# The output projection of a hybrid backbone layer, its operands split into float16 halves with power-of-two scales

## The chip, the core and the metric

The kernel runs on one core of one Trainium2 chip. The metric is device time in microseconds of one execution; a time is the median over the runs made. The engines are named as in the profile: PE multiplies matrices (PEld is its weight load, which runs beside it), DVE is the vector engine, ACT the scalar engine, POOL the GpSimd engine, SP the engine that issues most DMAs. Each engine takes its own instructions in the order in which they were written for it.

## What is computed

One layer over 4096 latent tokens of width 1024, with 256 context tokens ahead of them. An input projection gives eight groups of 512 columns: query q, two forget gates, value v, the gate g_a, the convolution's u and its gate, and the gate g_b. Two branches follow, and one output projection joins them:

```python
a_lat = rmsnorm(h_lat, norm_g[l]) * (1.0 + sc_l) + sh_l
q_l, zf_l, zb_l, v_l, ga_l, u_l, ug_l, gb_l = jnp.split(a_lat @ w_in[l], SPLITS, axis=-1)
...
branch_a = head_rmsnorm(o_hgrn, hgrn_norm_g_l) * jax.nn.silu(g_a)
branch_b = conv_y * jax.nn.silu(g_b)      # conv_y = silu(layernorm(depthwise conv of width 31))
out_lat = jnp.concatenate([branch_a, branch_b], axis=-1) @ w_out_l
...
h_lat = h_lat + gt_l * out_lat
return rmsnorm(h_lat, final_norm_g)
```

o_hgrn is a gated linear recurrence run forward and backward over the tokens; gt_l is a row of 1024 gates that depends on c alone. Everything is float32 in the reference.

## The kernel before

**Two stages.** Stage 1 walks forward over 16 blocks of 256 tokens. In a block, `hgrn` (the forward scan and the within-chunk scores), `row_conv` and the projections of the next block are interleaved by `merge`, which takes the next step of whichever generator is least far along; a scheduler then lists the instructions of each engine in the order in which they come ready in its own simulation, so that a DMA or a small step can move ahead of its place in the code. Results that stage 2 needs go to DRAM (`opd`, `qbd`, `ubd`, `yrd`, `gud`, `aTd`). Stage 2 walks backward over 32 groups of 128 tokens: `group_in` finishes the backward scan of a group (`pi`, `ps_c`, `ps_d`, `ps_o` are its PE steps), applies the norms and gates, and makes the operand of the output projection; `group_out` does the output projection of the group before it (`py`), the residual and the final norm; `gates` and `col_conv` of a later block run beside them.

**Splits.** Most matrix products run on two halves, high and low, in three passes (high by high, high by low, low by high; `PASSES`). For the input projection the halves are float16, with a power-of-two scale from the sum of squares (`exponent`, `split_chunk`). For the output projection (`split_wo` at line 896, the end of `group_in`, `group_out`) the halves are float32r: `yh = round(y)`, `yl = y - yh`, 4 bytes each. A group has 2 halves of 512 output columns x 3 passes x 8 chunks = 48 matmuls of 128x128 by 128x512.

**Side work.** A dictionary `side` (line 916) hangs preparation on blocks of stage 1: block 1 computes the gate row (`gate_rows`), block 2 measures the two gate weights (`scale_w2`: 8 loads of 512 KB, 8 squares on ACT, two small reductions through PE), blocks 3 to 6 split them (`split_w2`), blocks 7 to 10 fold gate and norm gain into w_out and split it (`split_wo`, two rows k per block, two halves each: two loads, a multiply on DVE, a copy on ACT, a subtract on DVE, two stores). Blocks 11 to 13 have no side work. The side tiles share the one buffer with tag "A" with the preparation of x two blocks ahead (`prep_rows`).

**Weights of stage 2.** `load_w2` loads the high halves of w_out (2 MB, into the place of weights no longer used) in block 15; the low halves, 4 MB in four DMAs from POOL's queue, are loaded at line 1175 into tiles of stage 2's own pool `m2`, which lies over the tiles of stage 1's pool `m1`.

`rsqrt` is one instruction on DVE and then 12 (for 4 columns) or 7 (for one column) small ones on POOL, in a chain.

## Time and profile before

| | |
|---|---|
| median of 3 runs | 2219.68 us (2218.23 to 2222.2) |
| the profiled execution's own time | 2215.77 us |
| its span, first to last instruction | 2214.0 us |
| PE / PEld busy in the span | 2083.6 us (94%) / 1642.5 us (74%) |
| DVE / ACT / POOL busy | 1749.6 (79%) / 996.3 (45%) / 458.5 us (21%) |
| mean granted PE clock | 0.978 of full speed |
| HBM read / written | 137.99 MB / 76.55 MB |

The profiled execution is a single one; 1.77 us of its time lie outside the span. Start times in the rows are microseconds from the span's start. Stage 1 ends near 1433, stage 2 runs from there to 2214. "idle before <- X" is time in which an engine stood still until X came.

### The profile page before, as it was taken

Reading aid. Unit: us, or ns where it says so; the run is one execution under the profiler, and the core shown is the slowest. Engines: PE = TensorE matmul, PEld = TensorE weight load, DVE = VectorE, ACT = ScalarE, POOL = GpSimd, SP = SyncE. Lnnn points to the kernel's source line nnn. Section 1 sums busy time; section 2 is a strip of 40 time slices with the busy share of each in tenths; the row PEclk is TensorE's granted clock in tenths of the full one; section 3 lists DMA queues with packets and bytes.
Section 4 is the critical chain, followed back from the end, with each engine's and each line's share of the span. In section 5 each row is a group of like instructions: output and inputs, shape, how many; then the busy total and the mean of one; then the engine's idle time right before and its main releaser. Section 6 shows DMA issues by size and latency. Waiting matters only on the chain. (4 is left out here: it accounts for less than half of the span.)

```text
span 2214.0 us, 54678 instructions
## 1 busy us (share of the span) xinstructions
PE 2083.6 (94%) x22334; PEld 1642.5 (74%) x22334; DVE 1749.6 (79%) x4270; ACT 996.3 (45%) x2310; POOL 458.5 (21%) x1146
## 2 busy tenths in 40 slices
PE   6999999999998999999999999978999999999997
PEld 3777778778777778778788876766677766667776
DVE  5988887897797887887898778888787887777754
ACT  4944545545535445445544543433333333333343
POOL 1110101110110110101110100044433344433332
PEclk8999999999999999999999999989999999999999
DMA  9436165324325335343322317332323322332322
GB/s 363 133 84 163 55 169 149 104 79 134 102 68 177 109 99 172 98 115 97 85 61 68 64 59 234 107 130 94 110 91 108 102 96 91 100 98 99 114 96 72
DMA packets 221476, 251.65 MB, mean 114 GB/s; under 512 B 143812, under 2 KB 147736, under 8 KB 216744
## 3 DMA queue, kind: packets, MB, share of 16 engines
q1 hardware_dynamic: 220104, 239.67, 36.4%
q0 software_dynamic: 1120, 8.49, 1.0%
q8 instruction: 175, 2.87, 0.5%
q14 instruction: 77, 0.63, 0.1%
HBM read 137.99 MB, written 76.55 MB: 97 GB/s over the span
## 5 line engine op out<-in xcount | busy, mean ns | idle before, releaser
L284 PEld LDWEIGHTS <-w 128*128 128x128 f16 x4704 | 455.8, 98 | 60.5 <-issue 2.6
L706 DVE SCALAR_TENSOR_TENSOR yr<-gu,convw,yr 128x224 f32<-128x224 f32 (+2 forms) x900 | 356.6, 444 | 0.0
L1048 DVE SCALAR_TENSOR_TENSOR ycs<-gu_all,convw,ycs 128x256 f32<-128x256 f32 (+2 forms) x828 | 343.9, 469 | 0.0
L284 PEld LDWEIGHTS <-pair 128*128 128x128 f16 x3168 | 308.5, 99 | 39.4 <-issue 0.6
L1146 PE MATMUL py<-wo,yh 128*128 128x512 f32 x1024 | 282.1, 413 | 3.8 <-ACT yh L1130 3.8
L81 POOL TENSOR_SCALAR xqh<-xssq 128x1 f32<-128x1 f32 x30 | 12.5, 418 | 1017.7 <-DVE xssq L257 1017.7
L1146 PEld LDWEIGHTS py<-wo,yh 128*128 128x128 f32 x1024 | 189.0, 192 | 43.8 <-ACT yh L1130 4.4
L284 PE MATMUL ps_z<-aT,pair 128*128 128x256 f16 x1632 | 191.1, 277 | 0.0
L1015 PE MATMUL ps_gb<-aT,w 128*128 128x256 f16 x1536 | 190.1, 273 | 0.0
L284 PE MATMUL ps_z<-aT,w 128*128 128x256 f16 x1632 | 188.3, 274 | 1.9 <-DVE aT L242 1.4
L295 PE MATMUL pv<-w,aT 128*128 128x512 f16 x816 | 184.4, 379 | 1.4 <-DVE gu L670 1.4
L751 ACT COPY km<-X 128x512 f32<-128x512 f32 x160 | 107.9, 675 | 168.2 <-DVE X L759 167.9
L284 PE MATMUL ps_u<-aT,w 128*128 128x256 f16 x1536 | 180.6, 274 | 0.0
L1003 PE MATMUL ps_ga<-w,aT 128*128 128x512 f16 x768 | 178.6, 385 | 0.0
L284 PE MATMUL ps_g<-aT,w 128*128 128x256 f16 x1536 | 178.3, 273 | 0.0
L284 PE MATMUL ps_q<-aT,pair 128*128 128x256 f16 x1536 | 172.9, 273 | 0.0
L1015 PEld LDWEIGHTS <-w 128*128 128x128 f16 x1536 | 145.5, 98 | 31.5 <-issue 15.8
L295 PEld LDWEIGHTS <-aT 128*128 128x128 f16 x816 | 77.4, 98 | 88.3 <-issue 1.6
L1146 PE MATMUL py<-wo,yl 128*128 128x512 f32 x512 | 139.6, 402 | 0.0
L1003 PEld LDWEIGHTS <-aT 128*128 128x128 f16 x768 | 72.8, 99 | 88.1 <-issue 10.4
L314 ACT ACTIVATE f<-f,lbv,oml 128x128 f32<-128x128 f32 x272 | 113.0, 485 | 0.1
L1146 PEld LDWEIGHTS py<-wo,yl 128*128 128x128 f32 x512 | 95.0, 192 | 19.1
(268 smaller groups left out, 3360.7 us busy)
## 6 DMA issues: line engine op xcount, KB each, us to landing
xt<-in_x_dram SPq DMA_DIRECT2D x64, 512.0 KB, 3.5
out_dram<-xt SPq DMA_DIRECT2D x31, 512.0 KB, 2.7
aTd<-aT SPq DMA_DIRECT2D x14, 1024.0 KB, 4.7
aT<-aTd SPq DMA_DIRECT2D x14, 1024.0 KB, 5.8
wst<-in_w_in_dram SPq DMA_DIRECT2D x16, 512.0 KB, 4.5
wod<-hl SPq DMA_DIRECT2D x32, 256.0 KB, 3.0
qbd<-X SPq DMA_DIRECT2D x31, 256.0 KB, 2.1
ubd<-ub SPq DMA_DIRECT2D x31, 256.0 KB, 2.0
```

What stands on the lines that cost most here:

```text
L81: eng.tensor_scalar(h, v, -0.5, 0.0, ALU.mult, ALU.add)
L284: nc.tensor.matmul(ps[:, j, :], w[:, wi, k, (ct + j) * P : (ct + j + 1) * P], aT[:, ai, k, :], start=n == 0, stop=n == 23)
L295: nc.tensor.matmul(pv, aT[:, ai, k, i * P : (i + 1) * P], W[G_V][:, wi, k, :], start=n == 0, stop=n == 23)
L314: nc.scalar.activation(fa, fa, AF.Identity, scale=oml[:, d, ct + j : ct + j + 1], bias=lbv[:, d, ct + j : ct + j + 1])
L706: nc.vector.scalar_tensor_tensor(ar[i][:, :, lo:hi], gr[i][:, :, lo + dl : hi + dl], convw[:, i, j : j + 1], ar[i][:, :, lo:hi], ALU.mult, ...
L751: nc.scalar.copy(fap(km, 0, kd), fap(Xs[gi], 0, ks))
L1003: nc.tensor.matmul(ps, aT[:, ai, k, i * P : (i + 1) * P], Wa[:, wi, k, :], start=n == 0, stop=n == 23)
L1015: nc.tensor.matmul(ps[:, j, :], Wb[:, wi, k, (ct + j) * P : (ct + j + 1) * P], aT[:, ai, k, :], start=n == 0, stop=n == 23)
L1048: nc.vector.scalar_tensor_tensor(ya, gu_all[:, i, (lo + dl) * GW : (hi + dl) * GW], convw[:, 2 + i, j : j + 1], ya, ALU.mult, ALU.add)
L1146: nc.tensor.matmul(py, y[:, k // 4, k % 4, :], W2[wi, nh][:, k, :], start=n == 0, stop=n == 23)
```

## The change

The halves of both operands of the output projection become float16. For that they need scales that keep them in float16's range: `wo_scales`, a new piece of side work in block 7, loads w_out once more, sums its squares, and works out from bounds (largest norm gains, gate weights' sums of squares, the shift and scale of the modulation, the largest gate) two power-of-two scales for y (`ky`), two for w_out (`kw`, `khg`), and one factor that undoes them (`kinv`). `gate_rows` gets two reductions for the largest and smallest gate. `split_wo` moves from blocks 7 to 10 to blocks 8 to 11, multiplies with the scale in every case, and stores both halves with one DMA of half the bytes. Both halves of w_out now lie together in DRAM (`wod[n]`, float16, 2 MB for each n) and come in with the two DMAs of `load_w2`; the four DMAs at line 1175 and their tiles are gone. In `group_in` the copies on ACT and the subtracts on DVE become scaled ones that write float16; in `group_out` the add of the residual becomes a multiply-add with `kinv`.

```diff
--- before.py
+++ after.py
@@ -142,7 +142,7 @@
     gtd = dr.tile([P, D], F32, tag="gtd", name="gtd")
     gsd = dr.tile([2, D], F32, tag="gsd", name="gsd")
     w2d = {g: [dr.tile([P, 2, 2 * 512], F16, tag=f"w2d{g}_{i}", name=f"w2d{g}_{i}") for i in range(4)] for g in (G_GA, G_GB)}
-    wod = [[dr.tile([P, KC, 512], F32, tag=f"wod{i}_{n}", name=f"wod{i}_{n}") for n in range(2)] for i in range(2)]
+    wod = [dr.tile([P, 2, KC, 512], F16, tag=f"wod{n}", name=f"wod{n}") for n in range(2)]
 
     def exponent(out_s, out_r, ssq):
 
@@ -157,6 +157,11 @@
 
     sc2 = const([P, KC, 2], name="sc2")
     rwall = const([P, 8, 2], name="rwall")
+    gmx = const([P, 2], name="gmx")
+    ky = const([P, 2], name="ky")
+    kw = const([P, 2], name="kw")
+    khg = const([P, 4], name="khg")
+    kinv = const([P, 1], name="kinv")
 
     def group_scale(ssq, g):
 
@@ -867,6 +872,8 @@
                 nc.tensor.matmul(pg, ones, acc[:, sl], start=True, stop=True)
                 nc.vector.tensor_tensor(bt[:, sl], bt[:, sl], pg, ALU.add)
             nc.sync.dma_start(gtd, bt)
+            nc.vector.tensor_reduce(gmx[:, 0:1], bt, AX.X, ALU.max)
+            nc.vector.tensor_reduce(gmx[:, 1:2], bt, AX.X, ALU.min)
             yield
 
         def scale_w2(g):
@@ -893,30 +900,93 @@
             nc.sync.dma_start(w2d[g][i], hl)
             yield
 
+        def wo_scales():
+
+            ssq = sm.tile([P, 8], F32, tag="ssq", name="ssq")
+            for k in range(KC):
+                t = e1.tile([P, D], F32, tag="xt", name="wst", bufs=2)
+                junk = e1.tile([P, D], BF16, tag="A", name="sqj")
+                nc.sync.dma_start(t, w_out[k * P : (k + 1) * P, :])
+                yield
+                nc.scalar.activation(junk, t, AF.Square, accum_out=ssq[:, k : k + 1])
+                yield
+
+            sq = sm.tile([P, 20], F32, tag="bsq", name="bsq")
+            for i, (v, n) in enumerate(((vec[:, R_HG : R_HG + 4], 4), (vec[:, R_LG : R_LG + 4], 4), (vec[:, R_LBI : R_LBI + 4], 4), (gv[:, 0, :], 8))):
+                nc.vector.tensor_tensor(sq[:, 4 * i : 4 * i + n], v, v, ALU.mult)
+            co = sm.tile([P, 6], F32, tag="bco", name="bco")
+            nc.vector.tensor_reduce(co[:, 0:3], sq[:, 0:12].rearrange("p (a b) -> p a b", b=4), AX.X, ALU.max)
+            nc.vector.tensor_reduce(co[:, 3:4], sq[:, 12:20], AX.X, ALU.max)
+            nc.vector.tensor_tensor(sq[:, 0:8], shv[:, 0, :], shv[:, 0, :], ALU.mult)
+            nc.vector.tensor_reduce(co[:, 4:5], sq[:, 0:8], AX.X, ALU.add)
+            nc.vector.tensor_reduce(co[:, 5:6], ssq, AX.X, ALU.add)
+            pb = ps_lv.tile([P, 512], F32, tag="lv", name="pb")
+            nc.tensor.transpose(pb[0:4, 0:P], co[:, 0:4], ident)
+            m4 = sm.tile([4, 1], F32, tag="bm4", name="bm4")
+            nc.vector.tensor_reduce(m4, pb[0:4, 0:P], AX.X, ALU.max)
+            dg = sm.tile([4, 4], F32, tag="bdg", name="bdg")
+            nc.vector.tensor_scalar(dg, ident[0:4, 0:4], m4, None, ALU.mult)
+            nc.tensor.matmul(pb[:, P : P + 4], ones[0:4, :], dg, start=True, stop=True)
+            nc.tensor.matmul(pb[:, P + 4 : P + 6], ones, co[:, 4:6], start=True, stop=True)
+            bc = sm.tile([P, 6], F32, tag="bbc", name="bbc")
+            nc.vector.tensor_copy(bc, pb[:, P : P + 6])
+            hg2, lg2, lb2, gv2, sh2, f2 = (bc[:, i : i + 1] for i in range(6))
+            yield
+
+            u = sm.tile([P, 2], F32, tag="bu", name="bu")
+            a2 = u[:, 0:1]
+            nc.vector.scalar_tensor_tensor(a2, gv2, 1024.0, sh2, ALU.mult, ALU.add)
+            nc.vector.tensor_scalar(a2, a2, ra[:, 0:1], 2.0 ** -27, ALU.mult, ALU.mult)
+            nc.vector.tensor_scalar(a2, a2, ra[:, 0:1], None, ALU.mult)
+            nc.vector.tensor_copy(u[:, 1:2], a2)
+
+            for i, g in enumerate((G_GA, G_GB)):
+                for _ in range(2):
+                    nc.vector.tensor_scalar(u[:, i : i + 1], u[:, i : i + 1], rwall[:, g, 1:2], None, ALU.mult)
+            nc.vector.tensor_scalar(u[:, 0:1], u[:, 0:1], 256.0, None, ALU.mult)
+            nc.vector.scalar_tensor_tensor(lb2, lg2, 512.0, lb2, ALU.mult, ALU.add)
+            nc.vector.tensor_scalar(u[:, 1:2], u[:, 1:2], lb2, 4.0, ALU.mult, ALU.mult)
+            ry = sm.tile([P, 2], F32, tag="bry", name="bry")
+            exponent(ky, ry, u)
+            g2 = sm.tile([P, 2], F32, tag="bg2", name="bg2")
+            nc.vector.tensor_tensor(g2, gmx, gmx, ALU.mult)
+            w2 = sm.tile([P, 2], F32, tag="bw2", name="bw2")
+            nc.vector.tensor_reduce(w2[:, 1:2], g2, AX.X, ALU.max)
+            nc.vector.tensor_scalar(w2[:, 1:2], w2[:, 1:2], f2, None, ALU.mult)
+            nc.vector.tensor_scalar(w2[:, 0:1], w2[:, 1:2], hg2, None, ALU.mult)
+            rv = sm.tile([P, 2], F32, tag="brv", name="brv")
+            exponent(g2, rv, w2)
+            nc.vector.tensor_tensor(rv, rv, ry, ALU.mult)
+            nc.vector.tensor_reduce(kinv, rv, AX.X, ALU.max)
+            nc.vector.tensor_scalar(kinv, kinv, 2.0 ** -28, None, ALU.mult)
+            c = sm.tile([P, 1], F32, tag="bc1", name="bc1")
+            nc.vector.reciprocal(c, kinv)
+            nc.vector.tensor_scalar(kw, ry, c, 2.0 ** -14, ALU.mult, ALU.mult)
+            nc.vector.tensor_scalar(khg, vec[:, R_HG : R_HG + 4], kw[:, 0:1], None, ALU.mult)
+            yield
+
         def split_wo(k):
 
             for n in range(2):
                 sl = slice(512 * n, 512 * n + 512)
                 gw = e1.tile([P, 2, 512], F32, tag="xt", name="gw", bufs=2)
-                hl = e1.tile([P, 2, 512], F32R, tag="A", name="hl")
+                hl = e1.tile([P, 2, 512], F16, tag="A", name="hl")
                 nc.sync.dma_start(gw[:, 0, :], gtd[:, sl])
                 nc.sync.dma_start(gw[:, 1, :], w_out[k * P : (k + 1) * P, sl])
                 yield
                 w = gw[:, 1, :]
-                if k < 4:
-                    nc.vector.scalar_tensor_tensor(w, w, vec[:, R_HG + k : R_HG + k + 1], gw[:, 0, :], ALU.mult, ALU.mult)
-                else:
-                    nc.vector.tensor_tensor(w, w, gw[:, 0, :], ALU.mult)
+                f = khg[:, k : k + 1] if k < 4 else kw[:, 1:2]
+                nc.vector.scalar_tensor_tensor(w, w, f, gw[:, 0, :], ALU.mult, ALU.mult)
                 nc.scalar.copy(hl[:, 0, :], w)
-                nc.vector.tensor_tensor(hl[:, 1, :], w, hl[:, 0, :].bitcast(F32), ALU.subtract)
-                for i in range(2):
-                    nc.sync.dma_start(wod[i][n][:, k, :], hl[:, i, :].bitcast(F32))
+                nc.vector.tensor_tensor(hl[:, 1, :], w, hl[:, 0, :], ALU.subtract)
+                nc.sync.dma_start(wod[n][:, :, k, :], hl)
                 yield
 
         side = {1: [gate_rows()], 2: [scale_w2(G_GA), scale_w2(G_GB)]}
         for i in range(4):
             side[3 + i] = [split_w2(G_GA, i), split_w2(G_GB, i)]
-            side[7 + i] = [split_wo(2 * i), split_wo(2 * i + 1)]
+            side[8 + i] = [split_wo(2 * i), split_wo(2 * i + 1)]
+        side[7] = [wo_scales()]
 
         W2, late = {}, {}
 
@@ -941,8 +1011,8 @@
                 columns(b)
             yield
             for n, old in ((0, G_U), (1, G_V)):
-                W2[0, n] = wp.tile([P, KC, 512], F32R, tag=f"w{old}", name=f"wo0{n}")
-                nc.gpsimd.dma_start(W2[0, n], wod[0][n])
+                W2["o", n] = wp.tile([P, 2, KC, 512], F16, tag=f"w{old}", name=f"wo{n}")
+                nc.gpsimd.dma_start(W2["o", n], wod[n])
                 yield
 
         N_W2 = 9
@@ -1119,16 +1189,16 @@
             yield
             for j in range(2):
                 nc.vector.tensor_tensor(yn[:, 2 * j : 2 * j + 2, :], yn[:, 2 * j : 2 * j + 2, :], d["gb"][j][:, :, tk], ALU.mult)
-            yh = m2.tile([P, 2, NH, P], F32R, tag="yh", name="yh", bufs=2)
-            yl = m2.tile([P, 2, NH, P], F32R, tag="yl", name="yl", bufs=2)
-            nc.scalar.copy(yh[:, 1], yn)
-            nc.vector.tensor_tensor(yl[:, 1], yn, yh[:, 1].bitcast(F32), ALU.subtract)
+            yh = m2.tile([P, 2, NH, P], F16, tag="yh", name="yh", bufs=2)
+            yl = m2.tile([P, 2, NH, P], F16, tag="yl", name="yl", bufs=2)
+            nc.scalar.activation(yh[:, 1], yn, AF.Copy, scale=ky[:, 1:2])
+            nc.vector.scalar_tensor_tensor(yl[:, 1], yn, ky[:, 1:2], yh[:, 1], ALU.mult, ALU.subtract)
             yield
             ps = ps_tr.tile([P, NH, P], F32, tag="tr", name="ps_o")
             for hd in range(NH):
                 nc.tensor.transpose(ps[:, hd, :], op[:, hd, :], ident)
-            nc.scalar.copy(yh[:, 0], ps)
-            nc.vector.tensor_tensor(yl[:, 0], ps, yh[:, 0].bitcast(F32), ALU.subtract)
+            nc.scalar.activation(yh[:, 0], ps, AF.Copy, scale=ky[:, 0:1])
+            nc.vector.scalar_tensor_tensor(yl[:, 0], ps, ky[:, 0:1], yh[:, 0], ALU.mult, ALU.subtract)
             d["y", g] = (yh, yl, xt)
             yield
 
@@ -1143,11 +1213,11 @@
                 n = 0
                 for y, wi in ((yh, 0), (yh, 1), (yl, 0)):
                     for k in range(KC):
-                        nc.tensor.matmul(py, y[:, k // 4, k % 4, :], W2[wi, nh][:, k, :], start=n == 0, stop=n == 23)
+                        nc.tensor.matmul(py, y[:, k // 4, k % 4, :], W2["o", nh][:, wi, k, :], start=n == 0, stop=n == 23)
                         n += 1
                         if n % 6 == 0:
                             yield
-                nc.vector.tensor_tensor(h[:, sl], py, h[:, sl], ALU.add)
+                nc.vector.scalar_tensor_tensor(h[:, sl], py, kinv, h[:, sl], ALU.mult, ALU.add)
                 junk = m2.tile([P, 512], BF16, tag="junk", name="jk")
                 nc.scalar.activation(junk, h[:, sl], AF.Square, accum_out=hs[:, nh : nh + 1])
             r = sm.tile([P, 1], F32, tag="hr", name="hr")
@@ -1169,10 +1239,6 @@
         merge((N_COL, col_conv(NB - 1, ds[NB - 1])), (N_GATE, gates(NB - 1, ds[NB - 1])))
         load_group2(NG - 1, ds[NB - 1])
         load_block(NB - 3, ds[NB - 3])
-        for n in range(2):
-            W2[1, n] = m2.tile([P, KC, 512], F32R, tag=f"wo1{n}", name=f"wo1{n}")
-            for k in range(0, KC, 4):
-                nc.gpsimd.dma_start(W2[1, n][:, k : k + 4, :], wod[1][n][:, k : k + 4, :])
         ycs = e1.tile([P, 2, 4, TB], F32, tag=f"aT{NB % 2}", name="ycs")
         fng = e1.tile([P, D], F32, tag="A", name="fng")
         fg1 = final_norm_g.rearrange("(o n) -> o n", o=1)
```

## Rows read from the trace of the kernel before

**Rows 1.** Busy us of each engine in two stretches of stage 2, granted clock, DMA share, GB/s

```profile
1534.00:2039.00 505.00, 482.92 (x2770) 357.27 (x2770) 401.65 (x1057) 176.87 (x496) 213.01 (x560) 0.98 0.30 98
2039.00:2165.00 126.00, 125.71 (x765) 96.61 (x766) 77.69 (x203) 49.93 (x139) 40.87 (x140) 1.00 0.31 102
```

**Rows 2.** The same view for the matmuls of line 1146 alone (PE, PEld)

```profile
1455.00:1534.00 79.00, 45.60 (x186) 35.81 (x186) 0.95 0.27 94
...
2039.00:2165.00 126.00, 68.18 (x253) 45.44 (x254) 1.00 0.31 102
```

**Rows 3.** Who PE waited for from 1600 to 2214: us, times, longest

```profile
PE ps_d L1111 <- ACT yn L1098: 18.3, 9, 2.4
```

**Rows 4.** Chain that ended last, merged pieces: start us, us, what

```profile
2045.24 1.39 PE py L1146 x6
...
2075.98 6.92 PE ps_ga L1003 x32
```

**Rows 5.** Groups of instructions by form: busy us, mean ns of one, idle before

```profile
L1146 PEld LDWEIGHTS py<-wo,yh 128*128 128x128 f32 x1024 | 189.0, 192 | 43.8 <-ACT yh L1130 4.4 <-issue 1.4
...
L1003 PEld LDWEIGHTS <-aT 128*128 128x128 f16 x768 | 72.8, 99 | 88.1 <-issue 10.4
...
L1125 DVE TENSOR_TENSOR yl<-yn,yh 128x512 fp32r<-128x512 f32 x32 | 22.0, 686 | 9.1 <-ACT yh L1124 9.1
...
L184 DVE SCALAR_TENSOR_TENSOR w<-raw,rwall,w 128x512 f16<-128x512 f32 x16 | 11.1, 745 | 0.0
...
L823 ACT ACTIVATE osb<-po,es 128x512 f32<-128x512 f32 x30 | 20.6, 686 | 43.1 <-PE po L818 37.5 <-DMA opd<-osb 5.4
...
L1130 ACT CAST yh<-ps_o 128x512 fp32r<-128x512 f32 x32 | 18.7, 586 | 13.4 <-PE ps_o L1129 13.4
...
L881 ACT ACTIVATE sqj<-wst 128x1024 bf16<-128x1024 f32 x8 | 8.4, 1056 | 11.0 <-DMA wst<-in_w_in_dram 7.1 <-DMA aT<-hl 3.9
```

**Rows 6.** PE in order of time, one block of the steady part of stage 2

```profile
1735.12 0.66 PE L1111 MATMUL ps_d<-ident,yn 128*128 128x128 f32 x4 [2.00 <-ACT yn L1098]
...
1741.58 1.64 PE L1146 MATMUL py<-wo,yl 128*128 128x512 f32 x6
...
1786.58 0.81 PE L1111 MATMUL ps_d<-ident,yn 128*128 128x128 f32 x4 [2.01 <-ACT yn L1098]
```

**Rows 7.** DVE in order of time, the same block

```profile
1749.14 0.16 DVE L1105 TENSOR_SCALAR osq<-osq 128x4 f32<-128x4 f32 x1
...
1758.44 0.69 DVE L1118 TENSOR_TENSOR ops<-ops,ga 128x512 f32<-128x512 f32 x1 [2.29 <-ACT ops L1117]
...
1775.12 0.15 DVE L78 TENSOR_SCALAR lnr<-ba 128x1 int32<-128x1 int32 x1
```

**Rows 8.** POOL and PE in order of time, where stage 2 begins

```profile
1433.20 2.21 POOL L1175 DMA_DIRECT2D wo<-wod  x4 [15.54 <-DVE ycs L1048]
...
1448.92 2.04 PE L1078 MATMUL pi<-s_b,qb 128*128 128x128 f32 x8 [9.87 <-DMA qb<-qbd]
1451.97 1.12 PE L1129 MATMUL ps_o<-ident,op 128*128 128x128 f32 x4 [1.01 <-DVE op L1118]
```

**Rows 9.** SP's queue in order of time: one such store pair per block of stage 1

```profile
278.09 1.03 SPq L806 DMA_DIRECT2D qbd<-X  x2
...
362.09 1.59 SPq L806 DMA_DIRECT2D qbd<-X  x2
...
604.64 5.18 SPq L806 DMA_DIRECT2D qbd<-X  x2
...
943.56 1.81 SPq L806 DMA_DIRECT2D qbd<-X  x2
...
1101.68 1.52 SPq L806 DMA_DIRECT2D qbd<-X  x2
...
1178.04 1.52 SPq L806 DMA_DIRECT2D qbd<-X  x2
```

**Rows 10.** The split of w_out, by its tile: what its engines waited for (us, times)

```profile
  DMA wod<-hl: 18.0, 8
```

## The prediction

> **What bounds the kernel now.** I read first the page's busy shares: PE is busy 94% of the span, DVE 79%. An average over stages says little, so the next view is the busy time by stretch [rows 1]. From 2039 to 2165 PE is busy 125.71 of 126 us at full clock: there every nanosecond taken from PE counts. From 1534 to 2039 it is busy 482.92 of 505 us, at a clock of 0.98, and the list of waits says why [rows 3]: nine waits of some 2 us, all of them PE at `ps_d` waiting for `yn`, the normed convolution, which ACT makes when POOL's chain for the inverse root is done.
>
> One such block in order of time shows what sets its length [rows 6, 7]. PE waits 2.00 us at 1735.12 and 2.01 us at 1786.58: a block of 51.46 us between two waits. From the first wait PE works 7.9 us, until the `py` group of 1741.58 ends and `pi` runs; from there the chain goes over DVE, ACT and POOL: the squares' reduction on DVE at 1749.14, the multiply at 1758.44 (DVE stood idle 2.29 us before it), then DVE without a gap until it hands the variance on at 1775.12, POOL's chain, `yn` on ACT, and the next `ps_d`. In that ring PE holds 7.9 of 51.5 us. The other PE work of the block runs beside it, with 2 us to spare.
>
> Stage 1 is read from the stores of `qbd`, of which each block makes one pair [rows 9]. A block without side work takes 1178.04 - 1101.68 = 76.4 us. The block that holds `scale_w2` takes 362.09 - 278.09 = 84.0 us. The four intervals that hold `split_wo` take (943.56 - 604.64) / 4 = 84.7 us each. Side work costs 7.6 to 8.3 us a block, though it needs almost nothing of PE.
>
> **The matmuls.** The float32r matmul runs at 1.39 / 6 = 231.7 ns between other work [rows 4]. The nearest float16 matmul of the same shape, `ps_ga`, runs at 6.92 / 32 = 216.3 ns [rows 4]. So 15.4 ns each, 1.48 us for a block's 96, and 1536 x 15.4 = 23.7 us if PE were the bound in all of stage 2.
>
> The weight load takes 192 ns for float32r and 99 ns for float16 [rows 5]. If the loads set the pace, 1536 x 93 = 143 us would come back; but the pace of 231.7 ns is longer than the load, so the load is already hidden behind the matmul before it. The Trainium skill, "TensorE: Matmul & The Clock Gate", section "Weight-path perf modes", has the fast weight load on for all types but fp32 and measured at about twice the speed; the trace agrees. Its page "Perfetto Trace Analysis" takes the busy share of the weight loads for a good measure of the distance from the roofline; by that the 143 us would be the sum here.
>
> *Stretch 2039 to 2165.* 253 matmuls [rows 2] x 15.4 = 3.9 us. A block here has no wait left, but the ring is close behind (the last wait of the list is at its start), and where it takes over the gain stops. Bounds 0 and -3.9; I take -2.5.
>
> *Stretch 1534 to 2039.* Nine blocks. If the order on the engines stays, only the `py` inside PE's part of the ring counts: 12 of them (6 before and 6 in the group at 1741.58), 12 x 15.4 = 0.18 us less. DVE's subtracts and adds get a per-partition scalar: 686 ns becomes 745 ns, from the nearest such form [rows 5]; some five of them lie in the ring, +0.3 us. That is +0.1 us a block: nothing is gained, PE only waits longer. At the other end the scheduler, which puts ready matmuls ahead of a `ps_d` that is not ready, moves work from behind the wait to before it, and the whole 1.48 us counts. I take -0.6 a block, nearer the first end since the ring is what the rows show: -5.4; bounds +1 and -13.3.
>
> *Start of stage 2.* 186 matmuls [rows 2] x 15.4 = 2.9 us, but a wait of PE on the same chain follows at 1534. The four DMAs of the low halves go: 4 MB, issued at 1433.20. PE's longest wait, 9.87 us for `qb`, falls into them [rows 8]. Removing them does not give that back: the next step, `ps_o` at 1451.97, waited for DVE's multiply, which hangs on POOL's chain and not on a DMA; `qb` early leaves PE idle to the same 1451.97. The tiles of `m2` also move in memory, so that their first loads wait for other tiles of stage 1. Bounds -4 (the matmuls and 1 us of `ps_o`) and +2; I take -1.5.
>
> *End.* After 2180 two groups of 48 matmuls stand on the path, 96 x 15.4 = 1.5 us. Against it, in the last group, the copy on ACT from PSUM with a scale costs 686 instead of 586 ns and the DVE multiply-adds 0.06 us each [rows 5]: -1.2 (bounds -1.5 and -1).
>
> Stage 2 in sum: -10.6.
>
> **The side work.** `wo_scales` is an added block of side work (7 to 11 instead of 7 to 10): 8 loads of 512 KB through SP and 8 squares of 1056 ns on ACT [rows 5], the same loads and squares as `scale_w2`, for which the block took 84.0 - 76.4 = 7.6 us more [rows 9]. Behind a square that waits for its load stand ACT's copies `km`, for which PE's `pl` waits; behind loads in SP's queue stand the transposes of K, for which PE's `pu` waits. Its reductions add some 45 DVE instructions of about 0.15 us, as short as the row at 1749.14 [rows 7], and two visits to PE, each of which waits for DVE's queue while PE's next matmuls stand behind it. Bounds: 4 us (half of that) and 11 us (half as much again, as its one reduction goes to PE twice and its DVE part is longer). I take +7.
>
> `split_wo` stores once instead of twice, at half the bytes. ACT waited 18.0 us in 8 places for the buffer that these stores hold [rows 10]. The store that frees it could not go before DVE's subtract and still cannot; only its bytes shrink. Bounds 0 and -6 (a third of the wait); I take -2. The two reductions in `gate_rows` hide in DVE's slack, 21% of the span (3.0 us if not: 1024 columns twice, at 745 ns for 512 [rows 5]); I take 0. Stage 1 in sum: +5.
>
> Total: -10.6 + 5 = -5.6 us. The profiled execution took 2215.77 (its span of 2214.0 and 1.77 around it), the median is 2219.68; the sum goes onto both: 2210.2 for a profiled one, 2214.1 for the median. A measurement of this kernel tells about 0.2%, 4.4 us, from no change.
>
> **The rivals.**
> *The whole saving arrives* (chance 0.14). The order adapts in every block: 23.7, less 0.3 for ACT and DVE at the end, less stage 1's 5: -18.4, 2201.3. For it: the 2 us that PE has to spare come from the order alone. Against: the ring's 44 us outside PE.
> *The two stages cancel* (0.27). Ring kept in nine blocks (+1 instead of -5.4): 2214.1 + 6.4 = 2220.5, no change.
> *The added block costs more* (0.19). The place: block 7, PE's two visits of `wo_scales` waiting for DVE, which is 79% busy over the span. With a price of +11 for the block, no gain in `split_wo`, the ring kept: 11 + 1 - 2.5 - 1.5 - 1.2 = +6.8, 2226.5. It decides from a block price of +9 on, the ring kept; if the ring moves as forecast it needs +15.
> *The weight loads set PE's pace* (0.01): 143 - 5 us less, 2082. Against it: 231.7 ns is longer than 192.
> *The wait for `qb` goes with the low halves' load* (0.01): 9.87 us more than forecast, 2204.2. Against it: `ps_o` at 1451.97 hangs on DVE.
> *My forecast* has 0.38.
>
> Faster: 0.38 + 0.14 + 0.01 + 0.01 = 0.54, less 0.02 for what of the forecast falls short of 4.4 us: 0.52. Same 0.27 + 0.02 = 0.29, slower 0.19. Range: from the first rival, 2201, to the third, 2226; beyond each lies about 0.1. The forecast's own range is 2208 to 2215.
>
> **What the profile after would show.** `py` at 216 ns in the chain and weight loads at 99 ns: the matmuls are right. Nine waits at `ps_d` of 3 us and blocks still near 51 us: the ring holds; waits of 2 us and blocks near 50: the order moved. One more stage-1 interval near 84 us, and `split_wo`'s near 84: the side work is as priced. Wrong would be the sum if stage 1's intervals shrink by more than 2 us each, or if the ring were set by PE.

## The result, and the profile after

The changed kernel takes 2197.32 us (median of 4 runs, 2192.60 to 2203.76) against 2218.95 us before: a ratio of 0.9904, 95% interval 0.9874 to 0.9933. It is faster by 21.6 us where 5.6 were forecast, and lies outside the range. The profiled execution takes 2195.34 us (span 2193.6).

By landmarks the 20.4 us between the two spans fall so. The last store of `qbd`, taken here as the end of stage 1, is at 1403.53 before and 1405.93 after: +2.4. From there to the `ps_d` of an odd group at 1582.80 (1582.98 after): -2.2. The nine steady blocks up to 2039.29 and 2021.66: 456.5 against 438.7, **-17.8**. The stretch behind them, up to 2132.63 and 2112.82: -2.2. The rest: -0.6. So most of the surprise is in the steady blocks: 1.98 us from each on the mean, where 0.6 were forecast.

The busy time by stretch, after (the columns are those of [rows 1]):

```profile
1535.00:2022.00 487.00, 465.20 (x2774) 281.53 (x2775) 407.69 (x1058) 181.27 (x500) 215.66 (x560) 0.99 0.32 102
2022.00:2145.00 123.00, 122.10 (x766) 77.13 (x765) 79.88 (x206) 49.73 (x136) 41.59 (x140) 1.00 0.32 104
```

PE is busy 465.20 of 487 us, 95.5%, the share that it had before in [rows 1] (95.6%): it did not become the bound. The list of waits from 1586 on (who waited for whom: us, times, longest) answers to [rows 3]:

```profile
PE ps_d L1181 <- ACT yn L1168: 18.2, 20, 1.6
```

The nine waits of 2 us are now two to a block, and their sum is unchanged. The steady blocks in order of time on PE, as [rows 6]:

```profile
1730.93 0.66 PE L1181 MATMUL ps_d<-ident,yn 128*128 128x128 f32 x4 [0.60 <-ACT yn L1168]
...
1755.40 0.66 PE L1181 MATMUL ps_d<-ident,yn 128*128 128x128 f32 x4 [1.56 <-ACT yn L1168]
...
1779.49 0.66 PE L1181 MATMUL ps_d<-ident,yn 128*128 128x128 f32 x4 [0.61 <-ACT yn L1168]
```

This block lasts 48.56 us (1779.49 - 1730.93), against 51.46 for the one of [rows 6]; the nine before last from 49.2 to 51.8 us, so the mean gain is less than this pair shows. And DVE, as [rows 7]:

```profile
1743.23 0.17 DVE L1175 TENSOR_SCALAR osq<-osq 128x4 f32<-128x4 f32 x1 [1.56 <-ACT jk L1174]
1743.48 1.28 DVE L1230 SCALAR_TENSOR_TENSOR xt<-xt,hr,fng 128x1024 f32<-128x1024 f32 x1
...
1750.99 0.69 DVE L1188 TENSOR_TENSOR ops<-ops,ga 128x512 f32<-128x512 f32 x1
...
1769.05 0.15 DVE L78 TENSOR_SCALAR lnr<-ba 128x1 int32<-128x1 int32 x1
```

Here is what the forecast had not looked for: **the instructions stand in another order.** After, the squares' reduction `osq` is issued ahead of the final multiply of `xt`; before, that multiply stood ahead of `osq` at 1749.14 [rows 7], behind a wait of 1.43 us for POOL's `hr`:

```profile
1747.94 1.28 DVE L1160 SCALAR_TENSOR_TENSOR xt<-xt,hr,fng 128x1024 f32<-128x1024 f32 x1 [1.43 <-POOL hr L85]
```

The multiply `ops` at 1750.99 has no idle time before it now; the 2.29 us of [rows 7] are gone. Nothing in the diff moves either instruction. It is not the only move: to turn one order into the other over six steady blocks (in the changed kernel from 1633.85 to 1924.84), 71 of DVE's 636 instructions, 96 of POOL's 336 and 56 of PE's 1680 have to change places (counted in the two traces by the tile that each writes).

The chain of work and the groups by form answer to [rows 4, 5]:

```profile
2051.24 5.61 PE py L1216 x26
2056.86 6.91 PE ps_ga L1073 x32
```
```profile
L1216 PEld LDWEIGHTS <-yh 128*128 128x128 f16 x1024 | 101.0, 99 | 108.2 <-issue 6.6 <-ACT yh L1200 4.7 <-ACT yh L1194 0.5
...
L1195 DVE SCALAR_TENSOR_TENSOR yl<-yn,ky,yh 128x512 f16<-128x512 f32 x32 | 23.9, 746 | 10.3 <-ACT yh L1194 10.3
...
L1200 ACT ACTIVATE yh<-ps_o,ky 128x512 f16<-128x512 f32 x32 | 21.8, 680 | 12.7 <-PE ps_o L1199 12.7
```

A `py` matmul takes 5.61 / 26 = 215.8 ns and its weight load 99; the scaled operations cost 746 ns on DVE and 680 on ACT. The prices of the forecast were right.

Two theories for the 17.8 us. **Pace:** the 1.48 us that a block's 96 matmuls save arrive, with something on top. **Order:** the scheduler, which sets the order on each engine from costs and due times of its own, came out with another order; that shortened the ring, the way over the engines from one `ps_d` to the next, whatever the matmul costs.

### The profile page after: what moved, and what is told of

It is laid out like the page before. It is cut to its first block, busy times and chain, and to the rows that moved or that the text cites. A ratio compares the mean times of both kernels' runs of the same rounds, so it can differ in the third digit from the quotient of the medians.

```text
span 2193.6 us, 54736 instructions
## 1 busy us (share of the span) xinstructions
PE 2062.3 (94%) x22339; PEld 1520.1 (69%) x22339; DVE 1764.1 (80%) x4315; ACT 1009.9 (46%) x2326; POOL 458.5 (21%) x1142
## 4 chain that ended last, share of the span: by engine, by line
DVE 38%; PE 26%; POOL 14%; issue 7%; DMA 7%; ACT 6%; SPq 1%; DVEq 0%; ACTq 0%; POOLq 0%
DVE yr L711 9%; PE py L1216 5%; PE ps_z L289 4%; DVE ycs L1118 4%; DVE X L764 3%; PE ps_g L289 2%; POOL xqt L84 2%; PE ps_q L289 2%; DVE X L763 2%; POOL lnrt L84 2%; PE ps_u L289 2%; PE ps_gb L1085 2%; POOL lnr L85 2%; POOL hrt L84 2%; DMA X<-K 1%
## 5 line engine op out<-in xcount | busy, mean ns | idle before, releaser
L289 PEld LDWEIGHTS <-w 128*128 128x128 f16 x4704 | 457.4, 99 | 61.9 <-issue 2.6
L1216 PE MATMUL py<-wo,yh 128*128 128x512 f16 x1024 | 251.4, 385 | 3.8 <-ACT yh L1200 3.8
L1216 PEld LDWEIGHTS <-yh 128*128 128x128 f16 x1024 | 101.0, 99 | 108.2 <-issue 6.6
L1085 PEld LDWEIGHTS <-w 128*128 128x128 f16 x1536 | 150.4, 98 | 29.3
L1216 PE MATMUL py<-wo,yl 128*128 128x512 f16 x512 | 128.7, 381 | 0.1
L1222 ACT ACTIVATE jk<-xt 128x512 bf16<-128x512 f32 x64 | 40.1, 627 | 116.2 <-DVE xt L1220 77.9
```

Source lines behind the costliest of these rows:

```text
L289: nc.tensor.matmul(ps[:, j, :], w[:, wi, k, (ct + j) * P : (ct + j + 1) * P], aT[:, ai, k, :], start=n == 0, stop=n == 23)
L1085: nc.tensor.matmul(ps[:, j, :], Wb[:, wi, k, (ct + j) * P : (ct + j + 1) * P], aT[:, ai, k, :], start=n == 0, stop=n == 23)
L1216: nc.tensor.matmul(py, y[:, k // 4, k % 4, :], W2["o", nh][:, wi, k, :], start=n == 0, stop=n == 23)
```

## Experiments: order or pace

**e1: the changed kernel with float32r put back.**
```diff
-    wod = [dr.tile([P, 2, KC, 512], F16, ...) for n in range(2)]
+    wod = [[dr.tile([P, KC, 512], F32, ...) for n in range(2)] for i in range(2)]
-            yh = m2.tile([P, 2, NH, P], F16, ...)
+            yh = m2.tile([P, 2, NH, P], F32R, ...)
```
(likewise `hl`, `yl`, the two loads and the operand of `py`)

> The changed kernel with one thing put back: the halves are float32r again, in both operands, with the 8 MB of weights and the two loads of low halves that go with them. The scales, the side work and the scaled operations stay, and DVE, ACT and POOL issue stage 2 in the changed kernel's order. Theory pace (the 15.4 ns of each of 96 matmuls reach the time, 1.48 us a block, and a stretch at half clock goes with them): the stage is as long as before, nine steady blocks of 50.2 us or more, 810 to 815 us from the last store of qbd to the end, 2214 to 2222 us in all. Theory order (the scheduler's other order of the squares' reduction and the final multiply shortened the way from one ps_d to the next, whatever the matmul costs): 789 to 797 us for the stage, 2196 to 2204 us in all.

Measured: 2203.22 us, ratio 0.9931 (0.9907 to 0.9955); stage 2 (last store to end) 2206.1 - 1412.1 = 794.0 us. PE in order of time, and its busy time over nine blocks:

```profile
1737.79 0.66 PE L1182 MATMUL ps_d<-ident,yn 128*128 128x128 f32 x4
...
1762.27 0.66 PE L1182 MATMUL ps_d<-ident,yn 128*128 128x128 f32 x4 [0.76 <-ACT yn L1169]
...
1786.47 0.66 PE L1182 MATMUL ps_d<-ident,yn 128*128 128x128 f32 x4
```
```profile
1592.00:2028.00 436.00, 429.24 (x2514) 318.63 (x2513) 369.50 (x954) 162.19 (x450) 194.48 (x503) 1.00 0.32 104
```

In six steady blocks e1 issues the instructions of PE, DVE, ACT and POOL in exactly the changed kernel's order. A block lasts 48.68 us with float32r matmuls, 0.12 more than with float16. The slower matmuls eat the wait (0.76 us a block instead of 0.60 + 1.56), PE is busy 98.5% of the time, and the block is as long. In these blocks float16 is worth 0.12 us of its 1.48. The 6.3 us by which its stage 2 is longer than the changed kernel's (787.7) lie ahead of the nine blocks and behind them; the nine themselves last 438.3 us, against 438.7.

**e2: the kernel before with the final multiply behind the squares' reduction.**
```diff
+                def last(c0=c0, c1=c1):
+                    nc.vector.scalar_tensor_tensor(h[:, c0:c1], h[:, c0:c1], r, fng[:, c0:c1], ALU.mult, ALU.mult)
+                    nc.sync.dma_start(out[g * P : (g + 1) * P, c0:c1], h[:, c0:c1])
...
-            nc.vector.tensor_scalar(sq, sq, 1.0 / P, EPS, ALU.mult, ALU.add)
+            osq = nc.vector.tensor_scalar(sq, sq, 1.0 / P, EPS, ALU.mult, ALU.add)
...
+            if g + 2 in fin:
+                with after(osq):
+                    fin.pop(g + 2)()
```
(the load of `xt` moves behind it)

> The kernel before with one thing moved: DVE issues the final multiply of a group behind the squares' reduction of the group two further on, as the changed kernel does; float32r operands, nothing scaled. Theory pace: no gain, 2214 to 2223 us, blocks of 50.2 to 51.8 us. Theory order: the nine steady blocks lose 12 to 17 us, 2201 to 2208 us in all.

Measured: 2191.20 us, ratio 0.9877 (0.9862 to 0.9893), blocks of 48.0 to 48.2 us. PE, then DVE in order of time:

```profile
1727.35 0.66 PE L1114 MATMUL ps_d<-ident,yn 128*128 128x128 f32 x4 [0.21 <-ACT yn L1096]
...
1775.39 0.66 PE L1114 MATMUL ps_d<-ident,yn 128*128 128x128 f32 x4
```
```profile
1738.67 0.17 DVE L1103 TENSOR_SCALAR osq<-osq 128x4 f32<-128x4 f32 x1 [1.56 <-ACT jk L1102]
1738.75 1.28 DVE L1165 SCALAR_TENSOR_TENSOR xt<-xt,hr,fng 128x1024 f32<-128x1024 f32 x1
```

By its median it is 6 us below the changed kernel, without one float16 operand of it; it has no scales to compute in stage 1 either, and its stage 2 of 791.0 us is 3.3 us longer than the changed kernel's. The gain lies beyond even the order theory's bounds. Against the order of before only 30 of DVE's 636 instructions, 24 of POOL's and 24 of PE's have changed places: this small move is enough.

**e3: the changed kernel with the squares' reduction behind the final multiply.**
```diff
-                nc.vector.scalar_tensor_tensor(h[:, c0:c1], h[:, c0:c1], r, ...)
+                fin[g] = nc.vector.scalar_tensor_tensor(h[:, c0:c1], h[:, c0:c1], r, ...)
...
-            nc.vector.tensor_scalar(sq, sq, 1.0 / P, EPS, ALU.mult, ALU.add)
+            with after(fin[g + 2]) if g + 2 in fin else ExitStack():
+                nc.vector.tensor_scalar(sq, sq, 1.0 / P, EPS, ALU.mult, ALU.add)
```

> The changed kernel with one thing moved: the squares' reduction waits on DVE behind the final multiply of the group two before, as in the kernel before; float16 operands stay. Theory pace: 2195 to 2200 us, blocks of 48.4 to 48.8 us. Theory order: the steady blocks are as long as before but for 0.6 us each, 2207 to 2216 us in all.

Measured: 2212.71 us, ratio 0.9972 (0.9960 to 0.9985). PE in order of time:

```profile
1735.92 0.74 PE L1182 MATMUL ps_d<-ident,yn 128*128 128x128 f32 x4 [1.94 <-ACT yn L1168]
...
1762.39 0.66 PE L1182 MATMUL ps_d<-ident,yn 128*128 128x128 f32 x4 [1.00 <-ACT yn L1168]
...
1787.19 0.82 PE L1182 MATMUL ps_d<-ident,yn 128*128 128x128 f32 x4 [2.19 <-ACT yn L1168]
```

The blocks are 51.0 to 51.3 us long again, with 2.9 to 3.2 us of wait in each; the nine of them last 458.3 us (1580.6 to 2038.9), 1.8 more than before. With the final multiply ahead of `osq` again the float16 kernel gains nothing in the steady blocks. The order as a whole is a third one, though: 90 of DVE's 636 instructions stand elsewhere than before, 96 elsewhere than after. Its profiled run is as long as that of before (2215.78 and 2215.77 us), with stage 1 longer by 5.9 us and the start of stage 2 shorter by 8.1; where the 6 us of its median lie, it does not show.

**e5 and e6: one scaled operation alone, on the kernel before.**
```diff
e5
-            nc.scalar.copy(yh[:, 1], yn)
+            nc.scalar.activation(yh[:, 1], yn, AF.Copy, scale=one)
e6
-            nc.vector.tensor_tensor(yl[:, 1], yn, yh[:, 1].bitcast(F32), ALU.subtract)
+            nc.vector.scalar_tensor_tensor(yl[:, 1], yn, one, yh[:, 1].bitcast(F32), ALU.mult, ALU.subtract)
```
(and the same for half 0; `one` is a column of ones)

> The kernel before with one edit: ACT writes the high halves yh with a multiplication by a column of ones instead of a plain copy; float32r operands, the weights and the side work as before. In its program the squares' reduction stands ahead of the final multiply of even groups, and behind it no longer, as in the changed kernel. Theory order: this edit alone, which takes no work away, gives the whole gain, blocks of 48.0 to 48.7 us and 2188 to 2202 us in all. Theory pace: nothing in it can make a block shorter, 2215 to 2223 us.

> The kernel before with one edit: DVE makes the low halves yl with a multiplication by a column of ones in the same instruction as the subtraction; float32r operands, all else as before. Here the program keeps the order of the kernel before, the final multiply of even groups ahead of the squares' reduction. Theory order: blocks of 51.2 to 51.9 us and 2216 to 2226 us in all, no gain. Theory operations (the scaled operations change when things are due, whatever the order): the gain appears here too, 2190 to 2205 us.

Measured: e5 2189.37 us, ratio 0.9879 (0.9860 to 0.9897), blocks of 47.9 us; e6 2216.93 us, ratio 1.0005 (0.9993 to 1.0016), blocks of 50.0 to 51.9 us. DVE in e5 and in e6:

```profile
1735.29 0.17 DVE L1107 TENSOR_SCALAR osq<-osq 128x4 f32<-128x4 f32 x1 [1.56 <-ACT jk L1106]
1735.37 1.28 DVE L1162 SCALAR_TENSOR_TENSOR xt<-xt,hr,fng 128x1024 f32<-128x1024 f32 x1
...
1742.87 0.71 DVE L1120 TENSOR_TENSOR ops<-ops,ga 128x512 f32<-128x512 f32 x1 [0.16 <-ACT ops L1119]
```
```profile
1741.21 1.28 DVE L1162 SCALAR_TENSOR_TENSOR xt<-xt,hr,fng 128x1024 f32<-128x1024 f32 x1 [1.43 <-POOL hr L85]
1742.42 0.16 DVE L1107 TENSOR_SCALAR osq<-osq 128x4 f32<-128x4 f32 x1
...
1751.72 0.69 DVE L1120 TENSOR_TENSOR ops<-ops,ga 128x512 f32<-128x512 f32 x1 [2.29 <-ACT ops L1119]
```

A multiplication by one, which costs ACT 677 ns where the copy took 586 [rows 5], makes the kernel 27 us faster, since the program comes out with another order, `osq` ahead in it. The subtract that costs DVE more leaves the old order, in six steady blocks instruction for instruction on PE, DVE, ACT and POOL, with its 1.43 and 2.29 us of idle time, and gains nothing. Order it is: e1, e2, e3, e5 and e6 all fall on its side. Why the scheduler's costs tip one way in e5 and the other in e6 was not tried.

## Experiments: where the pace went

**e7 and e8: a shorter ring, with float16 and with float32r.**
```diff
-            rsqrt(nc, sm, r, ba[:, 1:2], 1, "lnr")
+            rsqrt(nc, sm, r, ba[:, 1:2], 1, "lnr", steps=1)
```

> The changed kernel with the reciprocal root of the layer norm (lnr) made in one Newton step instead of three, so that part of the computation is left out and yn is ready some 2 us earlier in each group; the order on DVE stays that of the changed kernel. Theory ring (the way over POOL and ACT to ps_d is what a block of the changed kernel still waits for, and the matmuls' pace shows once it is shorter): the wait of 0.6 and 1.55 us at ps_d goes, blocks of 46.3 to 46.9 us, 2176 to 2184 us in all. If the block is set by something else: 48.3 to 48.7 us, 2193 to 2198 us.

> The same single Newton step in the first kernel of these (the changed kernel with float32r operands); part of the computation is left out here too. Theory ring: TensorE, busy for 429.2 of 436.0 us there, has only the 0.7 us a block to give that it waits at ps_d, blocks of 47.8 to 48.1 us; so between this kernel and the one of float16 1.3 to 1.5 us a block remain, the pace of 96 matmuls, which with the long ring were 0.15. If the matmuls' pace is not worth it with a free ring either: the two kernels' blocks stay within 0.3 us of each other.

Measured: e7 2165.55 us, ratio 0.9766 (0.9747 to 0.9785); e8 2187.08 us, 0.9861 (0.9836 to 0.9886). PE in order of time in e7, then the busy time of e8 (columns as in [rows 1]):

```profile
1739.75 0.64 PE L1181 MATMUL ps_d<-ident,yn 128*128 128x128 f32 x4
1761.44 0.60 PE L1181 MATMUL ps_d<-ident,yn 128*128 128x128 f32 x4
1785.74 0.64 PE L1181 MATMUL ps_d<-ident,yn 128*128 128x128 f32 x4
```
```profile
1585.00:2015.00 430.00, 430.00 (x2534) 321.48 (x2533) 369.77 (x960) 165.99 (x457) 155.41 (x433) 1.00 0.33 107
```

No `ps_d` of these waits; a block of e7 lasts 46.0 us. In e8 PE is busy for all of 430 us and a block lasts 47.5. The two have the same order in six steady blocks, and the difference is 1.5 us a block, the 1.48 of the forecast's arithmetic; stage 2 differs by 774.9 - 754.8 = 20.1 of the 23.7 us. So the pace is real, and the changed kernel gets nearly nothing of it in its steady blocks: there it goes into the two waits at `ps_d`.

Only this pair is clean. Against the changed kernel the order did not stay, though the expectation says that it would: 107 of DVE's 636 instructions change places, and e7 is 10 us faster than its expected range. How much of its 32 us the shorter chain on POOL gives by itself is not shown.

**The ring in pieces.** From the rows in time of PE, DVE, POOL and ACT between 1640 and 1850 one half block, from one `ps_d` to the next, is cut at the end of the later `yl`, at the start of `bs`, at DVE's first instruction for `lnr`, and at the end of POOL's `lnm` (medians, us, so the pieces add up to the sums only nearly; first the half that ends with the odd group's `ps_d`, then the other):

```
          yl done   bs     lnr   lnm end  ps_d    sum  | yl done   bs     lnr   lnm end  ps_d    sum  | block
before      7.69   3.36   4.03   10.06   1.57   26.71 |   6.39   8.05   3.09    6.55   0.86   24.93 | 51.64
after       6.55   3.02   4.09    9.57   0.86   24.09 |   7.87   6.26   3.03    6.42   0.87   24.46 | 48.55
e1          6.63   3.02   4.20    9.50   0.87   24.21 |   7.88   6.27   3.03    6.43   0.87   24.48 | 48.69
e3          8.58   3.02   3.94    8.15   0.87   24.56 |   9.02   4.89   4.36    7.33   0.86   26.47 | 51.03
e5          6.50   2.96   3.44   10.05   1.19   24.13 |   7.06   6.73   3.03    6.05   0.87   23.74 | 47.87
e7          7.40   3.80   3.43    4.87   2.19   21.69 |  10.13   6.25   3.03    4.01   0.88   24.30 | 45.99
e12        12.46   1.17   3.43    9.34   0.87   27.27 |   8.96   1.17   3.30    9.10   0.87   23.40 | 50.67
```

After and e1 agree to 0.12 us in every piece: the float16 matmul shortens none. Before and after differ in what DVE and POOL have queued ahead of each piece, and in the clock, which the next paragraph takes out. In e7 the last piece of the odd half is long (2.19 us) without a wait: `yn` is ready and PE has other work.

**The clock's part.** The table's row of before is mixed with something else. In that kernel two half blocks begin with the same wait, 2.00 us at 1735.12 [rows 6] and 2.01 us at 1889.78, in the same order of the engines. Behind the first the granted clock falls, behind the second it does not (PE in order of time, then the columns of [rows 1]):

```profile
1760.05 0.66 PE L1111 MATMUL ps_d<-ident,yn 128*128 128x128 f32 x4
...
1889.78 0.66 PE L1111 MATMUL ps_d<-ident,yn 128*128 128x128 f32 x4 [2.01 <-ACT yn L1098]
...
1913.09 0.66 PE L1111 MATMUL ps_d<-ident,yn 128*128 128x128 f32 x4
```
```profile
1735.50:1738.90 3.40, 3.40 (x12) 2.17 (x11) 3.40 (x9) 2.19 (x5) 0.00 (x0) 0.54 0.13 52
1890.20:1893.60 3.40, 3.40 (x23) 2.64 (x22) 3.40 (x9) 2.09 (x5) 0.00 (x0) 1.00 0.10 42
```

12 of PE's matmuls fall into the first stretch and 23 into the second, and the half lasts 24.93 us (1760.05 - 1735.12) against 23.31; the difference stands in the piece to `bs`, 8.04 against 6.42. So one fall costs 1.62 us. Five of the nine steady blocks of before hold one, about 8.1 us as an estimate from these rows. The changed kernel has one, in its first: that half lasts 26.77 us against 24.44 in e4, which has the same order and the full clock there. So about 6 of the 17.8 us are the clock, which stays up behind the shorter waits, and about 12 are the ring itself.

With the falls taken out, a block of before lasts 26.5 + 23.3 = 49.8 us and one after 24.1 + 24.5. The ring gets shorter in the half that ends with the odd group's `ps_d`; the other half, in which `osq` and the final multiply changed places, is 1.1 us longer than before. The whole order counts, then, and not only the place where it was first seen. The falls go with the order and not with the type: e1 has none in its nine blocks, with float32r, and e3 seven, with float16.

## Experiments: tries at a faster version, and the side work

**e9, e10, e11: less on POOL.**
```diff
e9, e10
-            nc.gpsimd.tensor_tensor(nm, ba[:, 0:1], r, ALU.mult)
-            nc.gpsimd.tensor_scalar(nm, nm, -1.0, 0.0, ALU.mult, ALU.add)
+            nc.gpsimd.tensor_scalar(nm, ba[:, 0:1], r, -1.0, ALU.mult, ALU.mult)
e10
+            rsqrt(nc, sm, r, ba[:, 1:2], 1, "lnr", steps=2)
e11
+            rsqrt(nc, sm, r, ba[:, 1:2], 1, "lnr", nc.vector)
```

> The changed kernel with POOL's two instructions for the bias of the layer norm (mean by reciprocal root, then by -1) as one; nothing is left out and the order on DVE stays. Theory ring: the way to ps_d loses one POOL instruction and its hand-over, 0.2 to 0.5 us a group, so 0.4 to 1.0 us a block come off the 2.15 us of wait at ps_d, blocks of 47.5 to 48.2 us, 2186 to 2195 us in all. If the way over POOL does not set the block: 48.5 us, 2195 to 2200 us.

> The kernel of the run just before with two Newton steps for the reciprocal root of the layer norm instead of three, so a part of the computation is left out. Theory ring: with one step the block came to 46.0 us and TensorE had no more to give; with two, half of that way is saved, blocks of 46.0 to 47.0 us, 2166 to 2182 us in all.

> The changed kernel with the reciprocal root of the layer norm and its bias on DVE, all three steps. On DVE each of its eight instructions takes some 0.15 us, but the program puts one or two instructions of the convolution (0.40 us each) between them, so that they span 6 to 7 us, against some 5 us on POOL behind the other root. Theory ring: the other root is alone on POOL now, ready 1 to 2 us sooner, and the layer norm 0 to 2 us later, so blocks of 47.5 to 49.5 us and 2187 to 2206 us in all; if instructions moved off the crowded POOL were the gain by themselves, 46.0 to 46.8 us and 2165 to 2180 us.

Measured: e9 2197.77 us, 0.9907 (0.9890 to 0.9924), blocks of 48.2; e10 2191.08, 0.9882 (0.9860 to 0.9904), 48.0; e11 2194.11, 0.9900 (0.9879 to 0.9920), 48.5 to 49.4. The block of e9 gave 0.35 us, less than expected, and its total nothing that shows; DVE's order did not quite stay either, with 42 of 636 instructions elsewhere. e10 missed by more: the ring of its odd half fell by 0.9 us (23.23), that of the other rose by 0.3 (24.76), where the way to the later `yl` grew from 7.87 to 9.72 us as DVE's order had changed again. In e11 PE waited for `yh` instead (15.3 us in 9 places).

**e12, e13, e14: more matmuls beside the way to `ps_d`.** Since e10 had missed, this asked whether the work that stands beside the way counts.
```diff
             rsqrt(nc, sm, ro, sq, NH, "or")
             yield
+            yield
...
-        N_IN = 7
+        N_IN = 8
```
(on the changed kernel, on the kernel before, and with e9's edit)

> The changed kernel with one more step in group_in between the squares and the transposes of yn, nothing left out. In its program TensorE has 33 matmuls py and 48 ps_gb between ps_c and ps_d of an even group (24 and 53 in the changed kernel), 1.95 - 0.55 = 1.4 us more work over the way through DVE, POOL and ACT; the odd group has its 36 and 40 as before. Theory cover (a block is TensorE's own work plus what the way from ps_c to ps_d lasts beyond the matmuls that the program puts in between): the wait of 1.55 us goes almost wholly, blocks of 47.0 to 47.4 us, 2180 to 2188 us in all. Theory length (only a shorter way over POOL helps): 48.4 to 48.7 us, 2194 to 2200 us.

> The kernel before with the same one more step, float32r operands and nothing else of the change. In its program an even group has 33 matmuls py and 48 ps_gb between ps_c and ps_d, an odd one 33 and 40 (36 and 44 before). Theory cover: the even group has no wait; the odd one waits at most as long as in the changed kernel, so blocks of 47.6 to 48.6 us, TensorE's own work and up to 0.7 us, 2183 to 2200 us in all, and this kernel without float16 is about as fast as the changed one. If the order is of no account: 2214 to 2222 us.

> The changed kernel with both the added step and the bias of the layer norm in one POOL instruction; nothing is left out. Its program has 31 matmuls py and 48 ps_gb in the even group, 33 and 40 in the odd one, 0.4 and 0.65 us less than with the added step alone. Theory cover: what the shorter way gives, 0.3 to 0.5 us, the scheduler takes back, blocks of 46.8 to 47.6 us, within 6 us of the kernel with the added step alone. Theory length: faster than that one by 5 us or more.

Measured: 2223.83 us, 1.0027 (1.0011 to 1.0043); 2224.78 us, 1.0035 (1.0018 to 1.0052); 2229.50 us, 1.0055 (1.0038 to 1.0072). All three are slower than the kernel before, and neither of the two theories holds. PE and DVE of e12:

```profile
1760.90 0.66 PE L1182 MATMUL ps_d<-ident,yn 128*128 128x128 f32 x4 [1.68 <-ACT yn L1168]
...
1788.18 0.66 PE L1182 MATMUL ps_d<-ident,yn 128*128 128x128 f32 x4 [2.59 <-ACT yn L1168]
```
```profile
1772.62 0.75 DVE L1202 SCALAR_TENSOR_TENSOR yl<-ps_o,ky,yh 128x512 f16<-128x512 f32 x1
...
1774.54 0.69 DVE L1159 BATCH_NORM_STATS2 bs<-ps_c 128x6 f32<-128x512 f32 x1
```

With the added step DVE gets to the second `yl` 11.7 us after the `ps_d` at 1760.90, behind instructions of the convolution; `bs` stands behind it, and with it the way to the next `ps_d`. The table's first piece is 12.46 instead of 6.55 us. More matmuls stood beside a way that had grown by more. A block follows the ring, and each edit deals the ring's order anew; which deal an edit brings could not be foretold from its size. That remains open.

**e4: without the computation of the scales.**
```diff
-            side[8 + i] = [split_wo(2 * i), split_wo(2 * i + 1)]
-        side[7] = [wo_scales()]
+            side[7 + i] = [split_wo(2 * i), split_wo(2 * i + 1)]
```
(with constants in `ky`, `kw`, `kinv`)

> The changed kernel without the computation of its scales: the four powers of two are constants that fit these inputs, the bounds on norms and gates are not computed, and the eight splits of the weights lie beside blocks 7 to 10 as before. Stage 2 is left as it was, 787 to 789 us in every theory. If the side work of the scales costs the 7 us that were forecast, and the splits saved less than the 2 us forecast for them, the last store of qbd is out at 1397 to 1400 us and the time is 2186 to 2191 us; if the scales cost only the 2.4 us by which stage 1 grew, it is out at 1402 to 1404 us, 2193 to 2196 us in all.

Measured: 2192.84 us, ratio 0.9882 (0.9864 to 0.9901); last store at 1400.3 us, stage 2 789.4 us. The run lies between its two expectations, and one profile of stage 1 does not settle a few us: the five profiles that have the stage 1 of before (before, e2, e5, e6, e13) have the last store at 1403.5, 1400.2, 1399.9, 1397.9 and 1405.5, mean 1401.4; the eight that have that of the changed kernel (after, e3, e7, e9 to e12, e14) at 1405.9 to 1410.4, mean 1408.2. So stage 1 costs about 6.8 us more, not the 2.4 of the one pair. Against e4 the scales would cost 1408.2 - 1400.3 = 7.9 us, and the splits, which e4 has in float16, give 1401.4 - 1400.3 = 1.1; but e4 is one profile, and by the medians it is 4.5 us faster than the changed kernel (2197.32 - 2192.84). How the 6.8 us divide is not settled.

## Why the prediction was wrong

- **The step that failed** is the stretch 1534 to 2039, in the words "If the order on the engines stays": -0.6 a block, with -13.3 in all as the far bound. The order did not stay, and the bound was no bound: it took the matmuls' saving for the most that a new order could give, while e2 and e5 gain 27 us by their medians (2218.72 - 2191.20, 2216.12 - 2189.37) with no faster matmul. What the runs show in its place: at full clock another order takes 1.3 us (the changed kernel) to 2.0 us (e5) from a block, and with its shorter waits the clock stays up, which gives another 1.6 us in those blocks where it fell. The forecast read the clock of 0.98 and gave it no term. With the final multiply ahead again (e3) the nine blocks change by +1.8 us, next to the forecast's end of +1. That the new order was a better one was luck: with that of e12 the nine blocks last 460.1 us, 3.6 more than before. Of the signs that the forecast named, waits of 2 us and blocks near 50 for an order that moved came nearest: 2.2 and 48.5.
- The ring was read rightly in this: PE waits at `ps_d` for a way over DVE, POOL and ACT, and a faster matmul only waits longer. After and e1 differ by 0.12 us a block. What the reading left out is that `osq` stood behind the final multiply and its wait for `hr`, a place that the order gave it and that e2 alone changes.
- Matmul 216.3 ns forecast, 215.8 measured; 15.4 x 96 = 1.48 us a block, 1.5 between e7 and e8. Weight loads of 99 ns and no 143 us: that rival is refuted, since between e8 and e7 stage 2 falls by 20.1 us, less than the matmuls' own 23.7. The Trainium skill, "Perfetto Trace Analysis", section "Identifying the Most-Contended Engine", judges TensorE's headroom by the matmul work done against the peak and by the weight loads' busy share. Here that share does not tell what there is to gain: between e1 and the changed kernel it falls from 73% (318.63 of 436 us) to 58% (281.53 of 487), and the block by 0.12 us.
- The stretch behind the steady blocks: -2.5 forecast, -2.2 measured. The end: -1.2 and -0.6. The start: -1.5 forecast, -0.7 up to the `ps_d` at 1534.13 (1535.84 after) and -1.5 in the block behind it. The wait for `qb` shrank from 9.87 us [rows 8] to 2.8, and the step behind it, `ps_o`, still started no earlier (1451.97 before, 1453.01 after), as forecast.
- Stage 2 in sum: -10.6 forecast, -22.8 measured (810.5 to 787.7 us).
- Stage 1: +5 forecast; +2.4 between the two profiles, +6.8 over the means. The added block of side work was put at +7 (4 to 11) and `split_wo` at -2 (0 to -6); e4's 7.9 and -1.1 lie inside these bounds, as far as one profile tells. The reading of `split_wo` was short, though: its last store is at 950.1, and the interval behind 943.56, which holds it, takes 82.1 us and was not counted.
- The rival "the whole saving arrives" named 2201.3 us, nearest to the result, by a mechanism that e1 refutes: without float16 stage 2 is 6.3 us longer, and not 23.7.

## What to carry to other kernels

Where a scheduler sets the order on the engines, an edit's effect is that of its operations plus that of the order which it happens to bring, and the second can be the larger by far: here -27 us from a multiplication by one (e5) and +26.5 us from an added step (e12 against the changed kernel, 2223.83 - 2197.32). So compare the order of the engines before anything is credited to the edit, and hold the new order fixed while the edit itself is undone, as e1 does. And compare blocks of the same granted clock: in the kernel before, two halves of one order differ by 1.62 us through the clock alone.

A faster operation beside the ring that sets a block was worth next to nothing here (0.12 of 1.48 us, e1); where PE's own work set the block it was worth its full arithmetic (e7, e8). The fastest kernels here that leave nothing out are e5 (2189.37 us) and e2 (2191.20 us), both without the float16 operands.

## What the runs showed of the hardware

The granted clock falls to its lower level behind some waits of PE and not behind others that are as long or longer: in the kernel before behind 2.00 us at 1735.12 and not behind 2.01 us at 1889.78, as shown above; in e3 behind 1.94 us at 1735.92, and in e12 not behind 2.59 us at 1788.18:

```profile
1736.40:1739.80 3.40, 3.40 (x10) 1.18 (x9) 2.56 (x7) 0.18 (x1) 2.53 (x9) 0.51 0.43 154
```
```profile
1788.70:1791.60 2.90, 2.90 (x16) 1.35 (x14) 1.94 (x5) 2.90 (x11) 0.00 (x0) 1.00 0.40 158
```

The first is at 1.2 GHz (0.51), the second at 2.4 GHz (1.00). What tells the two apart was not tried. Behind the changed kernel's waits of 0.6 and 1.56 us the clock stays at 1.00, so that part of its gain comes from there; the larger part does not, since e12 has a granted clock of 0.99 between 1640 and 1850 and blocks of 50.7 us there.

A float32r matmul of 128x128 by 128x512 takes 231.7 ns in a run of six [rows 4], 228 in e8's runs of 26, and its weight load 192 ns [rows 5]; in float16 they take 215.8 and 99 ns. The weight load is halved, and between e8 and e7 stage 2 gets no more than what the matmuls themselves save (20.1 of 23.7 us).
